# A list scheduler whose later work queues behind the last instruction of the first stage

## Chip, core and metric

One core of a Trainium2 chip runs the whole program. The metric is device time in microseconds of one execution, given as the median of the runs. Besides them one execution was profiled; its instruction records are the trace.

## What is computed

The reference is two layers of a diffusion backbone over 256 context and 256 latent tokens of width 1024 (512 rows of activations together). Each layer has a half-step feed-forward block, four token mixers side by side, and a second feed-forward block, each behind an RMS norm that is modulated by the conditioning vectors:

```python
def pre_norm(t, gain, m, i):
    return modulate(rms_norm(t, gain), m[..., 3 * i, :], m[..., 3 * i + 1, :])

def swiglu(h, w_up, w_down):
    a, g = jnp.split(h @ w_up, 2, axis=-1)
    return (jax.nn.silu(a) * g) @ w_down
...
# per layer: x + 0.5 * gate * swiglu(pre_norm(x)), then four mixers
# (gated DeltaNet, Hyena, Mamba-2 SSD, GLA), then the second feed-forward
```

The modulation `m` is the conditioning vector (one for context, one for latent) through a matrix `w_ada` of 1024 by 9 x 1024 per layer. The products run in float32 as three matmuls of split operands (high x high, high x low, low x high).

## The kernel before

The Python program does not emit instructions as it runs. A recording object (`Stand`) notes every operation with its engine, what it reads and writes, a modelled duration and a key, and `Plan.run` then lists them: on each of five queues (PE, DVE, ACT, POOL, SP) it takes at each modelled moment the operation with the smallest key among those whose inputs and buffers are ready. `build` emits the instructions in that order, and each engine runs its own queue strictly in order. All instructions are emitted by one statement, so the profile gives them line 585 (588 after the change), and tiles are told apart by name.

**The first stage** is `Kern.start` (line 792). It loads the tokens (`xin`, 8 transfers), transposes them, forms the RMS norm, and computes the modulation of the first norm in eight column blocks b0 to b7: four transfers `aw` of `w_ada` per block, 32 small matmuls (`px<-aw,cond`), an evacuation `adas`, two transposes, and three short DVE steps on the coefficients `c`. As block k is done, `norm_g` makes the normalised rows `hh` (ACT) and `hl` (POOL `v`, then DVE), and `up_mm(k)` issues the 12 matmuls of contraction block k of the first four column tiles of the feed-forward. Their weights come in four `raw` tiles of two transfers each (`load_w`); POOL makes the high part `wh`, DVE the low part `wl`. So the stage has 48 loads of 256 KB on SP and 96 matmuls of 512 columns. It ends with `up_evac`: `sil` (ACT), the product with the gate half (DVE), `ah` (ACT), `al` (DVE).

Within this stage the order on each queue is the order in which it is written: `manual_schedule` makes each operation depend on the one before it on its queue (`deps` of -1, which mean "not before it starts"; they order a queue and are no semaphore). When the block closes, `floor` is set to the recorder's clock, so everything stated later has a key that is no smaller. A key is only a priority, though: while the stage's next operation on a queue is not ready, a later one that is ready goes first.

**What is stated behind it** and is ready early: two small loads (`grp`, `cmats`); the generator `later()` in `body` (line 2477), with the Hyena filter inputs (`hy_load`, some thirty small transfers on the ACT queue together with `load_vA` and `load_layer`), the filter constants (`Fm`, `win`, `hywo`, `hyb` on SP) and the hidden layers of the filter network; the modulation of the other norms (`ada`, line 956), which streams `w_ada` in 256 KB tiles `aw` and accumulates them on DVE, eight steps `aa` per 512 KB; and the weights of the next feed-forward chunks (`wchunk`, line 686: one `raw` of 512 KB, `wh` on ACT, `wl` on DVE, three buffers of each), 24 matmuls of 512 columns a chunk.

The two lines that decide the order of all this are

```python
        if "SP" in self.strict:
            self.floor = self.t
...
        o.key = max(self.t - self.off[-1], self.floor)
```

Of the kernel before, what the change touches and what calls it, by code (L numbers as in the profile page):

```python
# [152 lines left out]
class Stand:  # L153
# [3 lines left out]
    def __init__(self, nc):  # L157
        self.real, self.shadow = nc, _bacc.Bacc("TRN2", target_bir_lowering=False, num_devices=1)
        self.ops, self.tiles, self.hist, self.dr = [], {}, {}, set()
        self.t, self.off, self.pe_last, self.maker = 0.0, [0.0], {}, {}  # L160
        self.strict, self.lead, self.floor = {}, 15.0, 0.0
        for a, e in self.ENG.items():
            setattr(self, a, self.Engine(self, e))

# [23 lines left out]
    @contextlib.contextmanager  # L188
    def manual_schedule(self, engines=None):

        self.strict = {NAMES[e]: None for e in engines}
        yield
        if "SP" in self.strict:
            self.floor = self.t
        self.strict = {}

    @contextlib.contextmanager
# [40 lines left out]
    def note(self, eng, name, args, kw):  # L238
        if name == "preload_act_table_set":
            return Note()  # L240
        o = Op()
        o.n, o.eng, o.name, o.args, o.kw = len(self.ops), eng, name, args, kw
        o.dma = name == "dma_start"
        o.deps, o.succ, o.new, o.tiles = {}, [], None, []
        aps = [x for x in list(args) + list(kw.values()) if isinstance(x, bass.AP)]
        o.func = None
        for x in list(args) + list(kw.values()):
            if isinstance(x, type(AF.Copy)):
                o.func = x
        for i, x in enumerate(aps):  # L250
            tn, w = x.tensor.name, i == 0
            if tn in self.tiles:
                b = self.box(x)
                if tn not in o.tiles:
                    o.tiles.append(tn)
                    if tn not in self.hist:
                        assert w, (tn, name)
                        o.new, self.maker[tn] = tn, o.n
                    else:

                        o.deps.setdefault(self.maker[tn], -1)
            elif tn in self.dr:
                b = self.dbox(x)
            else:
                continue
            self.access(o, tn, w, b, tn in self.dr)
            if w and eng == "PE":
                p = self.pe_last.get(tn)
                if p is not None:
                    o.deps[p] = max(o.deps.get(p, 0), 0)  # L270
                self.pe_last[tn] = o.n
        if eng in self.strict:
            if self.strict[eng] is not None:
                o.deps.setdefault(self.strict[eng], -1)
            self.strict[eng] = o.n
        for tn in o.tiles:
            self.tiles[tn][5] += 1
        self.cost(o, aps)
        o.key = max(self.t - self.off[-1], self.floor)
        if eng == "PE":  # L280
            self.t += o.occ / 1e3
        self.ops.append(o)
        return Note()
# [2247 lines left out]
```

## Time and profile before

| | |
|---|---|
| median of 3 runs | 2760.29 us (2759.2 to 2762.18) |
| profiled execution | 2761.68 us |
| its span, first to last instruction | 2759.9 us |
| PE busy, share of the span | 2661.1 us, 96% |
| DVE busy | 1910.1 us, 69% |
| ACT busy | 1043.5 us, 38% |
| POOL busy | 359.4 us, 13% |
| mean granted TensorE clock | 0.98 |

A busy PE here means that matmuls are in flight; the granted clock says at which of two speeds (1.0 is 2.4 GHz, 0.5 is 1.2 GHz). The 1.8 us between the profiled time and the span lie before the first and behind the last instruction. A wait is put down to the instruction or transfer that ended last before it.

### The profile page before, as it was taken

What the parts mean: (1) busy time and instruction counts of PE and PEld (TensorE: products, weight loads), DVE (VectorE), ACT (ScalarE), POOL (GpSimd) and SP (SyncE); (2) the same over time, 40 slices, a digit from 0 to 9 for tenths busy, and PEclk for the clock granted to TensorE, in tenths of its full rate; (3) what the DMA queues carried; (4) which work ended last, traced back from release to release, by engine and by line L of the source; (5) the groups of instructions that cost most, each with busy time, mean ns of one, the idle gap of its engine ahead of it and who ended that gap; (6) DMA issues with size and microseconds to landing.
All of it is one profiled execution on the core that took longest, in us unless ns stands there. A gap on an engine that the chain in (4) does not pass through costs nothing.

```text
span 2759.9 us, 40079 instructions
## 1 busy us (share of the span) xinstructions
PE 2661.1 (96%) x15131; PEld 2275.8 (82%) x15131; DVE 1910.1 (69%) x3783; ACT 1043.5 (38%) x1598; POOL 359.4 (13%) x439
## 2 busy tenths in 40 slices
PE   5999999999999999999999999999999899999998
PEld 3788877777989888887888878888878789999998
DVE  5968884778867565479737666556368987877555
ACT  2332222744433534233222233313246434644443
POOL 2200000201120242421000001000022112232000
PEclk6999999999999999999999999999999999999999
DMA  7745544232344233245534444444234435555454
GB/s 230 221 152 184 180 146 130 85 102 66 117 127 137 83 107 100 77 158 169 170 99 153 153 132 149 142 148 136 92 84 131 119 115 160 188 154 173 152 183 143
DMA packets 369697, 382.66 MB, mean 139 GB/s; under 512 B 43466, under 2 KB 317544, under 8 KB 369504
## 3 DMA queue, kind: packets, MB, share of 16 engines
q1 hardware_dynamic: 347568, 363.67, 43.3%
q10 hardware_dynamic: 21936, 16.44, 1.8%
q8 instruction: 119, 1.95, 0.3%
q14 instruction: 74, 0.61, 0.1%
HBM read 355.79 MB, written 24.25 MB: 138 GB/s over the span
## 4 chain that ended last, share of the span: by engine, by line
PE 83%; DVE 10%; DMA 3%; issue 1%; POOL 1%; ACT 1%; SPq 0%; ACTq 0%; DVEq 0%; POOLq 0%
PE pmm L585 72%; PE px L585 11%; DVE qkv L585 1%; DVE wl L585 1%; DVE X L585 1%; DVE P L585 1%; DVE xbc L585 1%; DVE aa L585 1%; DMA raw<-in_ffn_up 1%; DMA aw<-in_w_ada 0%; DVE u L585 0%; DMA gdr<-gA 0%; POOL bm L585 0%; POOL v L585 0%; DVE TC L585 0%
## 5 line engine op out<-in xcount | busy, mean ns | idle before, releaser
L585 DVE TENSOR_TENSOR wl<-raw,wh 128x1024 fp32r<-128x1024 f32 (+1 forms) x486 | 594.8, 1225 | 464.3 <-ACT wh L585 459.1
L585 ACT ACTIVATE wh<-raw 128x1024 fp32r<-128x1024 f32 (+1 forms) x480 | 502.0, 1046 | 1076.1 <-PE pmm L585 921.2
L585 PE MATMUL pmm<-hh,wh 128*128 128x512 f32 (+1 forms) x2464 | 896.2, 364 | 3.1 <-ACT hh L585 1.9
L585 PE MATMUL pmm<-hh,wl 128*128 128x512 f32 (+1 forms) x2464 | 886.7, 360 | 3.1 <-DVE wl L585 2.9
L585 PE MATMUL pmm<-hl,wh 128*128 128x512 f32 (+1 forms) x2464 | 885.2, 360 | 4.3 <-DVE hl L585 4.2
L585 PEld LDWEIGHTS pmm<-hh,wh 128*128 128x128 f32 x2464 | 469.4, 191 | 77.5 <-issue 8.6
L585 PEld LDWEIGHTS pmm<-hl,wh 128*128 128x128 f32 x2464 | 468.6, 190 | 74.8 <-DVE hl L585 7.1
L585 PEld LDWEIGHTS pmm<-hh,wl 128*128 128x128 f32 x2464 | 469.8, 191 | 70.5 <-DVE wl L585 4.4
L585 DVE SCALAR_TENSOR_TENSOR aa<-aw,cond,aa 128x256 f32<-128x256 f32 x896 | 369.8, 476 | 1.2 <-DMA aw<-in_w_ada 1.1
L585 PE MATMUL pmm<-ah,wh 128*128 128x512 f32 (+1 forms) x704 | 258.6, 367 | 0.0
L585 PE MATMUL pmm<-ah,wl 128*128 128x512 f32 (+1 forms) x704 | 256.4, 364 | 0.0
L585 PE MATMUL pmm<-al,wh 128*128 128x512 f32 (+1 forms) x704 | 256.2, 364 | 0.0
L585 PEld LDWEIGHTS pmm<-ah,wh 128*128 128x128 f32 x704 | 133.5, 190 | 23.0 <-issue 2.5
L585 PEld LDWEIGHTS pmm<-al,wh 128*128 128x128 f32 x704 | 133.3, 189 | 21.4 <-issue 0.4
L585 PEld LDWEIGHTS pmm<-ah,wl 128*128 128x128 f32 x704 | 133.5, 190 | 20.6
L585 PE MATMUL pmm<-wl,hh 128*128 128x256 f32 x416 | 119.7, 288 | 8.8 <-DVE wl L585 8.8
L585 PE MATMUL pmm<-wh,hh 128*128 128x256 f32 x416 | 120.3, 289 | 0.0
L585 PE MATMUL pmm<-wh,hl 128*128 128x256 f32 x416 | 119.6, 287 | 0.0
L585 POOL TENSOR_SCALAR v<-u,Am,mods 128x256 f32<-128x256 f32 x72 | 56.4, 804 | 466.9 <-DVE u L585 466.9
L585 PEld LDWEIGHTS pmm<-wl,hh 128*128 128x128 f32 x416 | 80.1, 193 | 9.4 <-DVE wl L585 9.0
L585 PE MATMUL pmm<-yh,wh 128*128 128x512 f32 (+1 forms) x256 | 87.8, 344 | 0.0
L585 PE MATMUL pmm<-yh,wl 128*128 128x512 f32 (+1 forms) x256 | 86.1, 338 | 0.0
(382 smaller groups left out, 3397.9 us busy)
## 6 DMA issues: line engine op xcount, KB each, us to landing
raw<-in_ffn_up SPq DMA_DIRECT2D x172, 512.0 KB
raw<-in_w_in SPq DMA_DIRECT2D x164, 512.0 KB
aw<-in_w_ada SPq DMA_DIRECT2D x288, 256.0 KB
raw<-in_ffn_down SPq DMA_DIRECT2D x80, 512.0 KB
raw<-in_w_branch SPq DMA_DIRECT2D x32, 512.0 KB
fe<-pk SPq DMA_DIRECT2D x42, 256.0 KB
raw<-in_w_out SPq DMA_DIRECT2D x16, 512.0 KB
pk<-pj ACTq DMA_DIRECT2D x26, 256.0 KB
```

The lines of the kernel that those rows point to most:

```text
L585: getattr(engines[o.eng], o.name)(*[sub(a) for a in o.args], **{k: sub(v) for k, v in o.kw.items()})
```

## The change

When the first stage closes, the recorder keeps the number of the last instruction that the stage put on each queue (`gates`). Every operation that is stated later gets a dependence of -1 on its own queue's one: the scheduler may not place it ahead of it. Nothing else is changed: keys, costs, buffers, the stage itself.

```diff
@@ -158,7 +158,7 @@
-        self.strict, self.lead, self.floor = {}, 15.0, 0.0
+        self.strict, self.lead, self.floor, self.gates = {}, 15.0, 0.0, {}
@@ -191,7 +191,8 @@
         self.strict = {NAMES[e]: None for e in engines}
         yield
         if "SP" in self.strict:
-            self.floor = self.t
+
+            self.floor, self.gates = self.t, dict(self.strict)
         self.strict = {}
@@ -269,6 +270,8 @@
                 self.pe_last[tn] = o.n
+        if self.gates.get(eng) is not None and eng not in self.strict:
+            o.deps.setdefault(self.gates[eng], -1)
         if eng in self.strict:
```

**SP, in the stage's loads.** Before, 18 transfers that belong to later work stand between the two halves of the stage's first weight tile (`raw_106`); these are the last ten of them, the second half, and the first load of block b1:

```order
L585 DMA cmats<-in_cmats 128x9x128
L585 DMA Fm_132<-in_dftF 128x512
L585 DMA win_134<-in_hywin 128x2x256
L585 DMA win_136<-in_hywin 128x2x256
L585 DMA hywo_138<-in_hy_wout 64x256
L585 DMA hywo_140<-in_hy_wout 64x256
L585 DMA hyb_144<-in_hy_bias 1x256
L585 DMA hyb_146<-in_hy_bias 1x256
L585 DMA hywo_138<-in_hy_wout 64x256
L585 DMA hywo_140<-in_hy_wout 64x256
L585 DMA raw_106<-in_ffn_up 128x2x256
L585 DMA aw_259<-in_w_ada 128x4x128
```

With the change the two halves (x2) stand together, behind the four loads of b0, and b1 and b2 follow at once:

```order
L588 DMA aw_99<-in_w_ada 128x4x128
L588 DMA raw_104<-in_ffn_up 128x2x256 x2
L588 DMA aw_225<-in_w_ada 128x4x128
L588 DMA aw_227<-in_w_ada 128x4x128
L588 DMA aw_229<-in_w_ada 128x4x128
L588 DMA aw_231<-in_w_ada 128x4x128
L588 DMA aw_233<-in_w_ada 128x4x128
```

Over the whole stage 32 transfers leave the places ahead of its last load: 17 `aw` tiles of 256 KB, 3 `raw` of 512 KB, `Fm` and `win` (4 of 256 KB), `cmats` (576 KB), `hywo` (4 of 64 KB) and three of a few KB.

**DVE, between two blocks of the stage.** Before, steps `aa` of the later modulation stand around the stage's `wl`, `c`, `u` and `hl` of one block:

```order
L585 SCALAR_TENSOR_TENSOR aa_352<-aw_391,cond_229,aa_352 128x256
L585 SCALAR_TENSOR_TENSOR aa_355<-aw_391,cond_229,aa_355 128x256
L585 TENSOR_TENSOR wl_578<-raw_277,wh_565 128x1024
L585 TENSOR_REDUCE c_588<-px_465 128x4
L585 TENSOR_TENSOR c_588<-c_588,vA_235 128x4
L585 TENSOR_SCALAR c_588<-c_588,vA_235 128x2
L585 TENSOR_TENSOR u_593<-x_239,px_449 128x512
L585 TENSOR_TENSOR hl_600<-v_574,hh_528 128x512
L585 SCALAR_TENSOR_TENSOR aa_358<-aw_391,cond_229,aa_358 128x256
```

With the change the same piece has none, and none stands anywhere in the stage:

```order
L588 TENSOR_TENSOR hl_366<-v_320,hh_317 128x512
L588 TENSOR_TENSOR wl_387<-raw_241,wh_375 128x1024
L588 TENSOR_REDUCE c_399<-px_299 128x4
L588 TENSOR_TENSOR c_399<-c_399,vA_170 128x4
L588 TENSOR_SCALAR c_399<-c_399,vA_170 128x2
L588 TENSOR_TENSOR u_406<-x_177,px_286 128x512
L588 TENSOR_TENSOR hl_411<-v_384,hh_361 128x512
```

88 steps `aa`, three `wl` of the next chunks, seven steps of the filter network and a copy of loaded rows move behind the stage's last DVE step.

**ACT, at the end of the stage.** Before, the first two splits of the next chunks (`wh_952`, `wh_1001`) stand among the stage's last evacuations, and all small transfers of `later()` far ahead of them:

```order
L585 ACTIVATE wh_952<-raw_671 128x1024
L583 ACT_TABLE_LOAD
L585 ACTIVATE sil_976<-pmm_505 128x512
L585 ACTIVATE sil_994<-pmm_540 128x512
L585 ACTIVATE wh_1001<-raw_737 128x1024
L585 ACTIVATE ah_1010<-sil_976 128x512
L585 ACTIVATE adas_1018<-px_870 128x256
L585 ACTIVATE ah_1038<-sil_994 128x512
```

With the change the splits stand behind the last evacuation, and the transfers between the splits that follow:

```order
L588 ACTIVATE ah_760<-sil_744 128x512
L588 ACTIVATE ah_765<-sil_751 128x512
L588 ACTIVATE wh_767<-raw_583 128x1024
L588 ACTIVATE wh_773<-raw_590 128x1024
L588 DMA hyz_783<-in_hyz 33x256
L588 DMA hyw_785<-in_hy_w 33x64
L588 DMA hyw_793<-in_hy_w 64x2x64
L588 DMA hyw_793<-in_hy_w 64x64
L588 ACTIVATE wh_809<-raw_665 128x1024
```

30 transfers now lie between `wh_773` and the split of the eighth chunk, `wh_1077`; 37 stood among the stage's instructions before. On PE two matmuls of the filter network, a transpose and seven picks (`px<-aa,pick`) move behind the stage, on POOL ten memsets. Behind the first feed-forward block the order on every queue is that of before, but for some dozens of neighbours that change places.

## Rows read from the trace of the kernel before

**Rows 1.** Busy time by stretch: PE, PEld, DVE, ACT, POOL (x), PEclk, DMA share, GB/s.

```profile
0.00:50.00 50.00, 20.29 (x136) 14.42 (x136) 21.38 (x56) 13.15 (x23) 10.20 (x25) 0.63 0.67 198
50.00:100.00 50.00, 42.47 (x307) 28.73 (x308) 43.11 (x102) 14.97 (x27) 23.03 (x18) 0.79 0.89 278
100.00:150.00 50.00, 50.00 (x221) 40.82 (x220) 48.50 (x101) 15.46 (x20) 0.00 (x0) 1.00 0.63 199
150.00:200.00 50.00, 50.00 (x223) 41.38 (x222) 28.60 (x51) 14.98 (x19) 0.00 (x0) 1.00 0.47 146
```

**Rows 2.** The chain that ended last, 0 to 110 us: start, us, what.

```profile
12.72 5.59 DMA raw<-in_ffn_up
18.33 8.29 DMA alog<-in_gdn_a_log
...
38.08 7.47 DMA aw<-in_w_ada
...
83.97 3.85 POOL wh L585
```

**Rows 3.** SP's queue: start, us, transfer.

```profile
35.73 0.59 SPq L585 DMA_DIRECT2D raw<-in_ffn_up  x1
```

**Rows 4.** Busy time by stretch, columns as in rows 1.

```profile
0.00:16.00 16.00, 7.35 (x31) 5.07 (x31) 3.97 (x8) 4.64 (x8) 6.00 (x20) 0.91 0.76 230
40.00:44.00 4.00, 0.66 (x8) 0.23 (x8) 0.00 (x0) 0.00 (x0) 1.04 (x1) 0.50 0.99 284
```

**Rows 5.** ACT's timeline: start, us, instruction, [idle before <- what ended it].

```profile
18.78 1.09 ACT L585 ACTIVATE sq<-px 128x512 f32<-128x512 f32 x2 [6.75 <-DMA rows<-in_gdn_conv]
```

**Rows 6.** PE's timeline through the stage to its last matmul.

```profile
23.64 3.54 PE L585 MATMUL px<-ones,acc 128*128 128x1 f32 x16 [2.23 <-DVE acc L585]
...
43.32 2.93 PE L585 MATMUL px<-aw,cond 128*32 128x128 f32 x32 [13.80 <-DMA aw<-in_w_ada]
...
52.26 0.80 PE L585 MATMUL pmm<-hh,wh 128*128 128x512 f32 x1
...
66.36 1.08 PE L585 MATMUL px<-aw,cond 128*32 128x128 f32 x32
...
70.59 0.43 PE L585 MATMUL px<-aw,cond 128*32 128x128 f32 x8
...
70.95 0.64 PE L585 MATMUL px<-hyh,hyw 64*64 64x256 f32 x2
...
75.89 0.80 PE L585 MATMUL pmm<-hl,wh 128*128 128x512 f32 x1 [2.19 <-DVE hl L585]
...
80.32 0.63 PE L585 MATMUL pmm<-hl,wh 128*128 128x512 f32 x1
...
100.22 0.39 PE L585 MATMUL pmm<-hl,wh 128*128 128x512 f32 x1
```

**Rows 7.** DVE's and ACT's steps of a gate product and of splits.

```profile
101.78 1.23 DVE L585 TENSOR_TENSOR wl<-raw,wh 128x1024 fp32r<-128x1024 f32 x1 [0.27 <-ACT wh L585]
...
103.53 0.68 DVE L585 TENSOR_TENSOR sil<-sil,pmm 128x512 f32<-128x512 f32 x1
...
104.24 0.63 ACT L585 ACTIVATE ah<-sil 128x512 fp32r<-128x512 f32 x1 [1.70 <-DVE sil L585]
...
228.34 1.06 ACT L585 ACTIVATE wh<-raw 128x1024 fp32r<-128x1024 f32 x1 [4.33 <-DVE aa L585]
233.78 1.06 ACT L585 ACTIVATE wh<-raw 128x1024 fp32r<-128x1024 f32 x1 [4.38 <-PE pmm L585]
```

**Rows 8.** PE's timeline in the feed-forward: a group of eight picks.

```profile
204.93 1.07 PE L585 MATMUL px<-aa,pick 128*32 128x256 f32 x16
```

**Rows 9.** ACT's queue: the first and the last of 37 small transfers of later work.

```profile
3.48 0.30 ACTq L585 DMA_DIRECT2D hyz<-in_hyz  x1
...
53.55 0.26 ACTq L585 DMA_DIRECT2D rows<-in_ssd_norm  x1
```

**Rows 10.** DVE's timeline: a run of modulation steps.

```profile
80.24 5.63 DVE L585 SCALAR_TENSOR_TENSOR aa<-aw,cond,aa 128x256 f32<-128x256 f32 x14
```

## The prediction

> **What bounds the kernel now.** The page's first line gives a span of 2759.9 us; the profiled execution took 2761.68, 1.4 above the median of 2760.29. I make the sum against the former and take the 1.4 off at the end. First read busy time by stretch [rows 1]: PE is busy for 20.3 of the first 50 us and 42.5 of the next 50, at a mean clock of 0.63 and 0.79; from 100 us on for 50.0 of 50 at full clock. The first stage is where PE waits, and the change acts there. The chain that ended last says why [rows 2]: from 12.72 us it runs through a `raw` of later work and through `alog`, a small transfer of later work on ACT's queue, 8.29 us, until SP could issue on; only at 38.08 does it reach a load of the stage. SP's queue has the second half of the first stage weight at 35.73 [rows 3], 23.0 us behind the start of that other `raw`, and PE stood 13.80 us for block b1 [rows 6]. Further on the chain passes POOL's `wh` with 3.85 us where it ran beside `aa` steps on DVE. So the moved work does not just fill gaps of the stage; it makes some of them.
>
> **The change, part by part.** First the stage's end without the moved work.
>
> *Loads.* The stage has 48 loads of 262 KB, 12.58 MB. In the first 16 us 230 GB/s moved [rows 4], 3.68 MB, just the 14 loads up to the first weight (3.67 MB). Block b1, four loads, now follows at once. A stretch with the stage's loads alone ran at 284 GB/s [rows 4], so b1 lands at 16 + 1.05 / 0.284 = 19.7 us and the last, b7, at 16 + 8.91 / 0.284 = 47.4, or at 54.7 with 230 GB/s.
>
> *The norm.* ACT stood 6.75 us before the row at 18.78, behind transfers of later work on its own queue [rows 5], in the middle of the sums of squares. That goes, and PE's norm matmuls, 23.64 to 27.2 [rows 6], end at 20.4. So b1's small matmuls, at 43.32 before, start at 20.4 rather than 19.7.
>
> *To the first weight matmul.* Before, from 43.32 to 52.26 [rows 6], 8.9 us; kept as it is: 29.3.
>
> *The eight blocks.* A chunk of 24 matmuls takes 233.78 - 228.34 = 5.44 us at full clock [rows 7], 0.227 each. Block 0 runs at half clock, 12 at 0.453 and two transposes, some 6.5 us, and I add 2.2 for a half-clock start of block 1. A block at full clock took 70.59 - 66.36 = 4.23 us [rows 6], its small matmuls included; five of them, 21.2. Blocks 6 and 7 have no small matmuls left: 12 matmuls and a little, 2.8 each, 5.6. Together 35.5, so the stage's last matmul is over at 64.8 instead of 100.4 (the row at 100.22 and one interval). b7 is needed at about 55, so loads and PE come out nearly even, and I take 66. **Gain 34.4 us.** Bounds: 60 with full clock from block 0 on; 77.5 if the stretch from 52.26 to 100.4 keeps its 48.2 us whole. I stay near the first, since the waits in that stretch are those named above.
>
> *The boundary.* The first `wh` of the next chunk now queues behind the last `ah`, and `wl` behind that. After the stage's last matmul come the gate product 0.68, `ah` 0.63, `wh` 1.06 and `wl` 1.23 [rows 7], 3.60 and with the handovers some 3.8 us, in which PE has two matmuls, 0.4: 3.4 lost. Before, nothing was lost there. After an idle 2.19 us PE ran at half clock from 75.89 to past 80.32, matmuls of 0.63 instead of 0.39 [rows 6]: 5 us for half as much work, 2.5 more. **5.9 us given back**; ends 3.4 and 8.
>
> *Work moved on PE.* Seven picks, two products of the filter network and a transpose stood in gaps and now stand in a full queue. Eight picks took 1.07 there [rows 8], one product 0.64 [rows 6], the transpose counts as a matmul of 0.4: **2.6 us**; the lower end is 0.
>
> *Work moved on DVE.* 88 steps `aa` of 0.40 in a run (5.63 for 14) [rows 10], 35 us, go into a stretch where DVE was busy for 48.5 of 50. Their cover is a lull: from 150 to 200 us it was busy for 28.6 of 50 [rows 1]. By the changed order DVE has, from the boundary up to the 23rd split, 199 `aa` (79.6), 23 `wl` (26) and some 11 us of gate products: 116 to 117. PE needs that split 22 chunks on, at 5.44: 119.7. So about 3 us to spare at the tightest place: **0**. By the 38th split as many `aa` are left as before. With the cover gone it would be up to 35 us.
>
> *Loads moved on SP.* 32 transfers, 7.9 MB, 27.9 us at 284 GB/s. The next two chunks' weights stand right behind the stage's last load; the third stands behind 2.6 MB more, 9.2 us, and is needed 10.9 us after the boundary. The loads are ahead of PE, so most of this lands while the stage still computes: **0**; ends 0 and 27.9. The Trainium skill speaks against this part: "DMA: Bandwidth & Descriptors", section "Rules for kernel authors", says to issue a DMA early and to wait for its semaphore late. By that rule the moved transfers are uncovered, and the whole gain would be spent on them; the trace shows the early issue as the cost [rows 2], as these transfers stood in line ahead of awaited ones.
>
> *Transfers moved on ACT.* 30 small ones now stand between the splits of chunks 2 and 8. Their issue takes 0.3 us and up [rows 9]. Seven chunks give ACT 38.1 us, less 2.1 for the first two splits, 6.4 for six more and 2.5 for four evacuations: 27.1, so 0.90 each are free. In the stage 37 of them went from 3.48 to 53.55 [rows 9], 1.36 each, with ACT's other work and full queues; at that, 30 x 0.46 = 14 us would be lost. The DMA share was 0.89 in the stage and is 0.63 behind it [rows 1], so I take **0**; ends 0 and 14.
>
> *POOL.* Ten memsets move behind its last stage step, where POOL has no work up to 200 us [rows 1]: 0.
>
> Sum: 34.4 - 5.9 - 2.6 = 25.9; 2761.7 - 25.9 = 2735.8, less 1.4 for the median: **2734.4 us**.
>
> **Rivals.** *ACT's queue starves PE a little.* A DMA issue can stand for earlier ones to land, as SP's did [rows 2]; at 1.2 to 1.36 us each 9 to 14 us go, and 2743 to 2748 is left. For it: the splits share that queue. Against: fuller queues then than now. *Slower*, at the same place, decided by the time per transfer: if each holds ACT for 1.95 us (30 x 1.05 = 31.5), the 25.9 are gone and 0.2% besides, 2766. One did stand for 8.29, but 1.36 on average with full queues speaks against. *Moved loads uncovered*: PE waits 27.9 us for `raw` in the first chunks, 2762. Against: PE's own work reaches to 66 us, the stage's loads to 55 at most. That is how it would go by the Trainium skill's rule named above. *Given back later*: `aa` steps run late and hold up DVE at the end of the feed-forward and at the next norm; 10 to 20 of their 35 us, 2745 to 2755. Against: the order behind that block is that of before. That the change does nothing is out: the order shows the moves.
>
> **How the numbers follow.** A measurement tells 0.2%, 5.5 us, from no change. The forecast with its bounds: 0.74. ACT a little late: 0.12. Given back later: 0.06, half of it within 5.5 us of before. Loads uncovered: 0.05, no change. Slower: 0.03. So faster 0.89, same 0.08, slower 0.03. Low end: a stage end of 60, 3.4 at the boundary, nothing on PE, 2723.3, taken as 2724. High end: ACT's 14 us with a stage end 4 us later, 2752.
>
> **What would show it.** SP: the stage weight's second half near 13 us, b7 issued by 50. PE: b1's small matmuls at 19 to 24, the first weight matmul near 30, the stage's last near 66, then a gap of 2.5 us and a short one, half clock for 5 us, and from there no wait to 400 us. POOL's `wh` near 1 us. All that follows is shifted as a whole. I am wrong if the stage ends behind 78 us, if PE waits for `wh` or `raw` between the boundary and 150 us, or if its waits behind 400 us grow by over 3 us.

## The result and the profile after

The changed kernel took 2733.07 us (median of 4 runs, 2732.03 to 2733.84) beside 2760.93 (4 runs) for the kernel before on the same chip: a ratio of 0.9899, 95% interval 0.9882 to 0.9916. That is 27.9 us less; 25.9 were forecast, and 2733.07 lies 1.3 us below the forecast of 2734.4. The profiled execution took 2733.53, with a span of 2731.4 us, 28.5 less than before. The steps were right in kind; two were off in size with opposite signs, and one came out partly by luck.

Busy time by stretch, after (columns: stretch, its length, busy us of PE, PE's weight load, DVE, ACT, POOL with the number of instructions, granted clock, DMA share, GB/s), beside [rows 1]:

```profile
0.00:50.00 50.00, 36.92 (x343) 28.67 (x344) 24.92 (x56) 15.45 (x32) 19.49 (x28) 0.86 0.99 302
50.00:100.00 50.00, 45.69 (x216) 36.44 (x215) 35.52 (x76) 18.20 (x28) 7.49 (x15) 0.93 0.58 174
100.00:150.00 50.00, 50.00 (x233) 40.21 (x232) 49.79 (x114) 16.73 (x22) 0.00 (x0) 1.00 0.67 212
150.00:200.00 50.00, 50.00 (x232) 40.10 (x231) 49.79 (x111) 12.78 (x17) 0.00 (x0) 1.00 0.68 210
```

In the first 50 us the loads run at 302 GB/s instead of 198, and PE works 36.9 us instead of 20.3. The lull of DVE from 150 to 200 us is filled (49.8 of 50), as the forecast had it for the 88 steps `aa`, and PE does not notice.

SP's queue, after (start, duration, what, how many):

```profile
9.09 1.63 SPq L588 DMA_DIRECT2D raw<-in_ffn_up  x2
10.76 7.65 SPq L588 DMA_DIRECT2D aw<-in_w_ada  x8
...
37.21 2.68 SPq L588 DMA_DIRECT2D aw<-in_w_ada  x4
```

Both halves of the first stage weight are issued by 10.7 us; the second stood at 35.73 before [rows 3]. The last block's loads are issued by 39.9. PE, after (an idle time before an instruction, and what ended it, in brackets):

```profile
20.59 1.93 PE L588 MATMUL px<-aw,cond 128*32 128x128 f32 x32
...
27.02 0.47 PE L588 MATMUL pmm<-hh,wh 128*128 128x512 f32 x1 [0.49 <-ACT hh L588]
...
30.80 0.80 PE L588 MATMUL pmm<-hl,wh 128*128 128x512 f32 x1 [2.77 <-DVE hl L588]
...
48.44 1.08 PE L588 MATMUL px<-aw,cond 128*32 128x128 f32 x32
52.65 1.08 PE L588 MATMUL px<-aw,cond 128*32 128x128 f32 x32
...
61.98 0.39 PE L588 MATMUL pmm<-hl,wh 128*128 128x512 f32 x1
66.11 0.88 PE L588 MATMUL pmm<-hh,wh 128*128 128x512 f32 x2 [3.75 <-ACT wh L588]
67.56 0.79 PE L588 MATMUL pmm<-hh,wl 128*128 128x512 f32 x1 [0.56 <-DVE wl L588]
68.15 0.63 PE L588 MATMUL pmm<-hl,wh 128*128 128x512 f32 x1
...
73.27 0.45 PE L588 MATMUL pmm<-hh,wh 128*128 128x512 f32 x1
```

Block b1's small matmuls start at 20.59, where they stood at 43.32 behind a wait of 13.80 us [rows 6]. Block 0 takes 8.8 us (27.02 to 35.80), blocks 1 to 5 take 4.21 each (52.65 - 48.44), and the stage is over at 62.2. Then comes the price: PE stands for `wh` and `wl`, 3.75 and 0.56 us, and up to 73.27 a matmul shows 0.63 us instead of 0.39, at a granted clock of 0.53 (columns as above):

```profile
66.11:73.27 7.16, 6.59 (x15) 4.76 (x16) 7.16 (x16) 1.96 (x2) 0.00 (x0) 0.53 0.61 179
```

All that lies further on is shifted as a whole. The kernel before, from 378 us to its end, and the one after, from 350:

```profile
378.00:2759.90 2381.90, 2320.29 (x13421) 2006.67 (x13419) 1620.15 (x3152) 938.23 (x1454) 325.61 (x396) 0.99 0.43 130
```

```profile
350.00:2731.40 2381.40, 2320.28 (x13420) 2007.11 (x13418) 1622.67 (x3152) 937.25 (x1454) 324.96 (x396) 0.99 0.43 130
```

The two rests are 2381.9 and 2381.4 us long, and PE is busy for 2320.3 in both. So nothing is given back later.

### The profile page after: what moved, and what is told of

Read it like the earlier page. It is cut to its first block, busy times and chain, and to the rows that moved or that the text cites. A ratio compares the mean times of both kernels' runs of the same rounds, so it can differ in the third digit from the quotient of the medians.

```text
span 2731.4 us, 40099 instructions
## 1 busy us (share of the span) xinstructions
PE 2652.9 (97%) x15131; PEld 2274.0 (83%) x15131; DVE 1910.5 (70%) x3783; ACT 1040.4 (38%) x1596; POOL 352.5 (13%) x439
## 4 chain that ended last, share of the span: by engine, by line
PE 69%; DVE 9%; POOL 1%; issue 1%; ACT 1%; DMA 0%; ACTq 0%; DVEq 0%; POOLq 0%; SPq 0%
PE pmm L588 60%; PE px L588 10%; DVE qkv L588 1%; DVE wl L588 1%; DVE X L588 1%; POOL v L588 1%; DVE P L588 1%; DVE xbc L588 1%; DVE aa L588 1%; POOL bm L588 0%; ACT wh L588 0%; DVE TC L588 0%; DVE u L588 0%; DVE Y L588 0%; ACT vn L588 0%
## 5 line engine op out<-in xcount | busy, mean ns | idle before, releaser
L588 ACT ACTIVATE ah<-sil 128x512 fp32r<-128x512 f32 (+1 forms) x88 | 49.3, 572 | 102.1 <-DVE sil L588 93.7
```

The source lines that it names most:

```text
L588: getattr(engines[o.eng], o.name)(*[sub(a) for a in o.args], **{k: sub(v) for k, v in o.kw.items()})
```

## The experiments

Six kernels are the changed one with one more condition on the gate; the line that this replaces is shown once. The last two have other edits. All were timed beside the kernel before on their chip: it took 2761.14 us on that of the runs with the gate on DVE, on ACT's transfers, on SP and on all transfers, and 2760.64 on that of the others. The last four columns are read from the one profiled execution of each kernel.

| gate | median us (range) | ratio, 95% interval | b1's small matmuls | first weight matmul | stage ends | GB/s, first 50 us |
|---|---|---|---|---|---|---|
| none (before) | 2760.93 | | 43.32 | 52.26 | 100.4 | 198 |
| DVE alone | 2755.69 (2752.28 to 2759.57) | 0.9983 (0.9973 to 0.9992) | 41.86 | 52.26 | 83.7 | 199 |
| ACT's transfers alone | 2743.43 (2741.14 to 2747.57) | 0.9942 (0.9927 to 0.9957) | 27.70 | 35.19 | 81.5 | 294 |
| SP alone | 2734.09 (2730.75 to 2735.15) | 0.9904 (0.9890 to 0.9919) | 25.45 | 36.40 | 69.0 | 224 |
| all (the change) | 2733.07 (2732.03 to 2733.84) | 0.9899 (0.9882 to 0.9916) | 20.59 | 27.02 | 62.2 | 302 |
| all but DVE | 2734.89 (2732.68 to 2736.41) | 0.9905 (0.9889 to 0.9922) | 21.39 | 27.21 | 61.7 | 316 |
| all transfers, nothing else | 2726.05 (2723.91 to 2727.02) | 0.9876 (0.9862 to 0.9891) | 20.57 | 27.01 | 61.4 | 312 |
| all but `wh` and `wl` | 2724.80 (2724.61 to 2727.33) | 0.9873 (0.9859 to 0.9888) | 20.12 | 26.56 | 62.2 | 323 |

Where the next matmuls follow without a gap, the stage's end is counted: from block 5 on as in the changed kernel, with the last 24 matmuls at 0.227 us.

### SP alone

```diff
-        if self.gates.get(eng) is not None and eng not in self.strict:
+        if eng == "SP" and self.gates.get(eng) is not None and eng not in self.strict:
```

> The gate holds for SP alone. Theory L (the gain of 28 us comes from transfers of later work that stood in line ahead of the stage's loads, most of it from SP's own 32): the stage weight's second half is issued by 14 us, but ACT's small transfers still stand among its squares, so b1's small matmuls start at 24 to 30 instead of 20.6 and the stage's last matmul ends at 67 to 75 instead of 62.2; the later splits may go ahead again, so the gap of 4.3 us at the boundary and the half clock behind it are gone (7.6 us back). Together 2730 to 2740. Rival A (ACT's small transfers are the main cause, through their wait on SP's queue of 8.29 us and the squares' 6.75): the stage ends behind 80, 2745 or more. Rival D (the 88 steps aa on DVE are the main cause): they can't run without their loads, so 2725 to 2735 too; this run does not tell D from L.

Measured: 2734.09 us. b1 at 25.45 and the stage's end at 69.0 lie in the ranges of theory L. The gap at the boundary is gone, since `wh` and `wl` go ahead again. So the 6.8 us that the stage is longer are about made up by the 7.5 that the boundary no longer takes, and the time equals that of the whole change. On ACT's queue the squares still stand behind a transfer, and PE's first weight matmul waits for the norm:

```profile
17.48 1.08 ACT L588 ACTIVATE sq<-px 128x512 f32<-128x512 f32 x2 [5.76 <-DMA hyv<-in_hy_freq]
```

```profile
36.40 0.76 PE L588 MATMUL pmm<-hh,wh 128*128 128x512 f32 x1 [4.25 <-ACT hh L588]
```

SP's queue holds nothing but the stage's loads in their right order, and still the loads come at 224 GB/s. Its waits in the first 65 us (sum, times, longest):

```profile
SPq L588 <- DMA aw<-in_w_ada: 14.9, 13, 3.7
SPq L588 <- DMA raw<-in_ffn_up: 4.6, 4, 2.7
```

With ACT's transfers held back too, in the whole change, the first of these is all but gone:

```profile
SPq L588 <- DMA aw<-in_w_ada: 0.4, 1, 0.4
```

### ACT's transfers alone

```diff
+        if eng == "ACT" and o.dma and self.gates.get(eng) is not None and eng not in self.strict:
```

> The gate holds for ACT's transfers alone. Theory L: the squares' wait of 6.75 us goes and so does SP's 8.29 us behind one of the small transfers, but 18 later transfers of SP still stand ahead of b1's loads and 14 more among the rest: b1's small matmuls at 31 to 38 instead of 43.3, the stage ends at 86 to 95 instead of 100.4, 2747 to 2756. Rival A: b1 near 24, stage end near 70, 2728 to 2738. Rival D: the aa steps are still in the stage, so the time of before less a few us, 2753 to 2760.

Measured: 2743.43 us, between the two theories; b1 and the stage's end come sooner than theory L had them. The 18 later transfers still stand ahead of b1 on SP, but they pass fast now:

```profile
14.08 0.33 SPq L588 DMA_DIRECT2D Fm<-in_dftF  x1
14.45 0.43 SPq L588 DMA_DIRECT2D cmats<-in_cmats  x1
15.79 0.80 SPq L588 DMA_DIRECT2D Fm<-in_dftF  x1
...
23.23 0.41 SPq L588 DMA_DIRECT2D raw<-in_ffn_up  x1
```

The weight's second half is issued at 23.23 instead of 35.73, and b1 starts 15.6 us sooner than before. I had expected 5 to 12. So ACT's small transfers cost SP's queue far more than their bytes. The two queues in the first 60 us of the kernel before, SP's and ACT's (packets, MB, share of the 16 engines' time):

```profile
q1 hardware_dynamic: 14986, 12.33, 66.7%
q10 hardware_dynamic: 4204, 0.46, 5.3%
```

From its first weight matmul on, though, this run's stage takes 46.3 us, nearly the 48.2 of before; the whole change takes 35.2. PE waits four times for `hl`, 1.98, 2.17, 1.46 and 1.74 us, where the whole change has one such wait. This is the part of rival D that holds. Runs of `aa` stand among DVE's work, POOL's `wh` takes 3.89 us beside one of them (1.04 to 1.05 in the whole change, which has none there), and `wl` and `hl` come late:

```profile
62.86 5.62 DVE L588 SCALAR_TENSOR_TENSOR aa<-aw,cond,aa 128x256 f32<-128x256 f32 x14
66.55 3.89 POOL L588 TENSOR_SCALAR wh<-raw 128x1024 fp32r<-128x1024 f32 x1 [7.42 <-DMA aw<-in_w_ada]
70.48 1.23 DVE L588 TENSOR_TENSOR wl<-raw,wh 128x1024 fp32r<-128x1024 f32 x1 [0.94 <-POOL wh L588]
73.36 0.50 PE L588 MATMUL pmm<-hl,wh 128*128 128x512 f32 x1 [1.74 <-DVE hl L588]
```

The two queues' parts do not add up. Against before, b1 comes 15.6 us sooner without ACT's transfers, 17.9 without SP's and 22.7 without both. The compiled program's listing says why. The transfers of both queues take eight semaphores in turn, and nearly every one in the stage waits until the transfer that had its semaphore last has landed. In the kernel before these three, on SP, ACT and SP, had the same one:

```
L585 DMA raw_110<-in_ffn_up 128x4x256 [waits DMAHW3_49]
L585 DMA alog_256<-in_gdn_a_log 128x2x4 [waits DMAHW3_49]
L585 DMA Fm_132<-in_dftF 128x512 [waits DMAHW3_49]
```

That is the chain of [rows 2] step by step: the `raw` from 12.72 us on, `alog` at 18.33 for 8.29 us, and SP's next issue at 26.63. A small transfer waits for a large one of the other queue, and the next large one for the small. Taking either party out ends most of it. How much of the stall is the turn-taking, and how much the slow landing of the small ones as such, was not separated.

### DVE alone

```diff
+        if eng == "DVE" and self.gates.get(eng) is not None and eng not in self.strict:
```

> The gate holds for DVE alone: no step aa is left in the stage. Because their tiles are then not freed, 12 of the 17 later loads aw are held back as well; the first 18 later transfers of SP and all of ACT's stay where they were. Theory L: b1's small matmuls start at 40 to 45 as before; from there on the stage runs with a few later loads in its way, some 4.3 to 5 us a block, and ends at 80 to 90; the later wl stand behind the stage's last DVE step, so half of the gap at the boundary stays. 2745 to 2758. Rival D: the aa steps were the cause, so most of the gain is here: 2728 to 2738.

Measured: 2755.69 us, in theory L's range. Rival D is out as the cause of most of the time: with no `aa` in the stage b1 is nearly as late as before, behind a transfer, and the first weight matmul as late to the hundredth:

```profile
41.86 0.65 PE L588 MATMUL px<-aw,cond 128*32 128x128 f32 x8 [11.13 <-DMA aw<-in_w_ada]
...
52.26 0.80 PE L588 MATMUL pmm<-hh,wh 128*128 128x512 f32 x1
...
89.40 0.80 PE L588 MATMUL pmm<-hh,wl 128*128 128x512 f32 x1 [2.02 <-DVE wl L588]
```

From there on the stage takes 31.4 us instead of 48.2, less than in any other run here, and PE waits for no `hl`. Two things are gone together: the `aa` steps, and 12 later loads whose tiles the held steps do not free. No run has one without the other, so what each is worth is not shown. Of the 16.7 us by which the stage is shorter, waits of 0.74, 1.34 and 2.02 us at the boundary, with half clock behind them, take some 7, and the work moved on PE some 2; the median is only 5.5 below that of before, so some 2 us stay open.

### All transfers, nothing else

```diff
+        if o.dma and self.gates.get(eng) is not None and eng not in self.strict:
```

> The gate holds for transfers alone, SP's and ACT's; nothing is held on DVE, PE, POOL or for ACT's arithmetic. Theory L: the stage as with the whole change (b1 at 20.6, last matmul at 62 to 64), and the splits wh and wl of the next chunks go ahead, so the gap of 4.3 us and 3.3 us of half clock are gone: 2724 to 2729. Rival D: aa steps may stand in the stage again and slow it: 2733 or more. Rival C (part of the gain comes from holding back the splits themselves, that is from ACT and DVE in the stage): 2731 to 2740, with b6 or b7 late by 1 to 3 us.

Measured: 2726.05 us, as theory L had it, 7.0 less than the whole change. The stage is that of the change to 0.8 us, the gap is gone, and PE is never idle from 50 to 100 us:

```profile
50.00:100.00 50.00, 50.00 (x251) 41.04 (x250) 42.28 (x89) 21.95 (x31) 3.92 (x4) 1.00 0.68 201
```

So holding back the two queues of transfers is enough for the whole gain. It keeps `aa` out of the stage as well, since their loads then come behind the stage's; this run does not tell the two apart.

### All but `wh` and `wl`

```diff
+        if aps[0].tensor.name.rstrip("0123456789") not in ("wh", "wl") and self.gates.get(eng) is not None and eng not in self.strict:
```

> The whole change, but the outputs wh and wl of later chunks are exempt from the gate; steps aa, transfers, picks and POOL's memsets stay held. Theory L (the boundary's gap comes from the splits alone): stage as with the change, last matmul at 62, no gap and no half clock behind it, 7.6 us less than the change's 2733.1: 2724 to 2728, the same as with the gate on transfers alone. Rival B (the gap is only shifted: the next chunks' raw or DVE's queue is late instead, and PE stops for it before 150 us): 2729 to 2733.

Measured: 2724.80 us, 8.3 less than the change, and the same as the last run within their ranges. On ACT two `wh` of the next chunks, at 55.11 and 57.29, stand ahead of the stage's last evacuations again:

```profile
57.29 1.05 ACT L588 ACTIVATE wh<-raw 128x1024 fp32r<-128x1024 f32 x1
60.34 1.28 ACT L588 ACTIVATE sil<-pmm 128x512 f32<-128x512 f32 x2 [2.01 <-PE pmm L588]
```

Rival B is out: its PE waits for nothing from 60 to 350 us. The boundary's price is that of the splits held back: 8.3 us by this run, and 7.0 by the one with the gate on all transfers, whose stage ends 0.8 sooner.

### All but DVE

```diff
+        if eng != "DVE" and self.gates.get(eng) is not None and eng not in self.strict:
```

> The whole change, but nothing is held on DVE; PE's order is that of the change to the last instruction. 8 steps aa stand ahead of the stage's first gate product and 9 more between the products and the first wl. Theory L (holding DVE earns nothing inside the stage, since the loads of aa come late anyway): the stage ends at 62 as with the change; at the boundary the products and so ah, wh and wl come up to 4 us later: 2733 to 2738. Rival D (holding aa back is what made the stage short): stage end behind 66, 2739 or more.

Measured: 2734.89 us, in theory L's range. The stage ends at 61.7 with DVE free to place `aa` in it, but none starts before 58.00, as their loads come behind the stage's; so this run says nothing of `aa` amid the stage. Eight steps stand ahead of the first gate product, and PE's gap grows from 3.75 to 5.70 us:

```profile
58.00 4.54 DVE L588 TENSOR_SCALAR aa<-aw,cond 128x256 f32<-128x256 f32 x8
62.47 0.67 DVE L588 TENSOR_TENSOR sil<-sil,pmm 128x512 f32<-128x512 f32 x1
63.07 1.66 DVE L588 SCALAR_TENSOR_TENSOR aa<-aw,cond,aa 128x256 f32<-128x256 f32 x4
```

```profile
67.59 1.22 PE L588 MATMUL pmm<-hh,wh 128*128 128x512 f32 x2 [5.70 <-ACT wh L588]
```

The 1.8 us between the medians is of that size, but the ranges overlap; it is the trace that shows the gap.

### Thirty more transfers on ACT behind the stage

```diff
-        self.strict, self.lead, self.floor, self.gates = {}, 15.0, 0.0, {}
+        self.strict, self.lead, self.floor, self.gates, self.twice = {}, 15.0, 0.0, {}, 0
...
         self.ops.append(o)
+        if self.gates and not self.strict and eng == "ACT" and o.dma and self.twice < 30 and aps[0].tensor.name in self.tiles and aps[0].ap[-1][1] > 2:
+            self.twice += 1
+            d = self.dram_tensor(f"tw{self.twice}", tuple(k for _, k in aps[0].ap), F32).ap()
+            self.note(eng, name, (d, aps[1]), {})
         return Note()
```

> The whole change, with 30 more small transfers on ACT's queue behind the gate: the first 30 of the later ones that move more than 2 elements a row are issued a second time, into scratch memory that nobody reads. This doses the term that I put at 0 with an upper end of 14 us. Theory L (a transfer behind the stage costs ACT 0.3 to 0.5 us, and 27 us are free in the next seven chunks, after which more chunks offer as much): PE waits nowhere for wh between the boundary and 200 us, 2732 to 2736. Rival A2 (ACT's queue was just short of its limit; each transfer stands 0.9 to 1.3 us for earlier ones): 2743 to 2765, with PE waiting for wh.

Measured: 2730.70 us (2729.57 to 2735.46), ratio 0.9896 (0.9881 to 0.9911): no cost. ACT does stand behind transfers, up to 6.91 us at once, and yet PE's waits from 60 to 350 us are those of the boundary alone:

```profile
74.53 1.06 ACT L592 ACTIVATE wh<-raw 128x1024 fp32r<-128x1024 f32 x1 [6.91 <-DMA hyw<-in_hy_w]
```

```profile
PE pmm L592 <- ACT wh L592: 3.8, 1, 3.8
PE pmm L592 <- DVE wl L592: 0.7, 1, 0.7
```

Three splits stand ahead of that wait, which gives PE some 16 us of work (3 x 5.44). The term I had put at 0 is 0 at twice the dose, but by this lead and not by short waits.

### The first `hl` sooner, with the gate on transfers

```diff
-        if self.gates.get(eng) is not None and eng not in self.strict:
+        if o.dma and self.gates.get(eng) is not None and eng not in self.strict:
...
-        ng = self.norm_g(lambda k: coef[k], 0, 512)
+        ng = self.norm_g(lambda k: coef[k], 0, 512, 2)
...
-        mod_t(1)
         load(3)
...
             next(ng)
+            if k == 0:
+                mod_t(1)
```

> The gate on transfers alone, and in the stage the first hl is stated ahead of two products u and of b1's coefficients, which stood before it on DVE; PE's order is unchanged. With the change, and with the gate on transfers, PE waits 2.8 us for this hl at 28 to 30.8 us and then runs at half clock to 35 us. Theory L: hl is there 1.5 to 2 us sooner, the wait is 1 us, b2 and all behind it are 2 to 3 us earlier: 2722.5 to 2725 against 2726.05 with the gate on transfers alone. Rival: block 1's hh or hl is late instead, by the coefficients that now come later: 2726 to 2728.

Measured: 2722.47 us (2720.93 to 2724.47), ratio 0.9863 (0.9849 to 0.9878), the fastest here: 10.6 less than the change, 38.2 less than before. PE's wait for this `hl` falls from 2.8 to 1.48 us:

```profile
29.55 0.56 PE L588 MATMUL pmm<-hl,wh 128*128 128x512 f32 x1 [1.48 <-DVE hl L588]
...
33.85 1.08 PE L588 MATMUL px<-aw,cond 128*32 128x128 f32 x32
```

The small matmuls of the block after start at 33.85, against 35.02 with the gate on transfers alone. The trace gives 1.2 us to this edit, less than the 2 to 3 expected; the medians differ by 3.6 with ranges that overlap, so more than the 1.2 is not shown.

## Why the prediction was right, point by point

**What bounds the stage.** It was read rightly from the chain of waits: transfers of later work in line ahead of awaited ones. Of the 38.2 us that the stage is shorter, 25.2 lie ahead of the first weight matmul (52.26 to 27.02), and those are shown to be SP's and ACT's transfers: with DVE alone held back that matmul stands where it stood. The other 13.0 lie behind it (48.2 to 35.2). There the forecast's last thread counts, POOL's `wh` beside `aa`: before, PE waited 2.19 us at 75.89 [rows 6] and 1.97 at 90.74 for `hl`, each behind a long `wh`, of 2.92 us in the row below and of 3.85 in [rows 2], and 2.9 for `aw` as well:

```profile
69.70 2.92 POOL L585 TENSOR_SCALAR wh<-raw 128x1024 fp32r<-128x1024 f32 x1 [6.55 <-DMA raw<-in_ffn_up]
```

```profile
90.74 0.50 PE L585 MATMUL pmm<-hl,wh 128*128 128x512 f32 x1 [1.97 <-DVE hl L585]
```

How these 13.0 divide between `aa` and the later loads is not shown. What the forecast did not see is that the two queues were one chain through their semaphores, and that 302 GB/s would run over 50 us; I had taken 284 and 230 [rows 4].

**The stage's end.** Said: 64.8, taken as 66. It is 62.2. b1's small matmuls start at 20.59 (20.4 said). The step that was off is "To the first weight matmul", kept at its 8.9 us of before: it takes 6.4 (27.02 - 20.59). The two groups of 32 small matmuls in it, spread over 2.86 and 3.33 us before by waits for single `aw` tiles, take 1.86 and 1.64, as b1 and b2 have landed; in the second the granted clock is 0.94 besides, where it was 0.50. That is 2.5, and the 1.2 for safety the rest. The eight blocks take 35.2 us (35.5 said), but their start came out by luck: 6.5 us of half clock for block 0 and 2.2 for a slow start of block 1 were said, 8.7 together. Block 0 did take 8.8, of which 2.77 are a wait for `hl` that was not foreseen, and block 1 began at full clock. Gain 38.2 instead of 34.4.

**The boundary.** Said: 3.4 idle and 2.5 of half clock, 5.9. Measured: 4.31 idle, and at half clock from 66.11 to 73.27 fifteen matmuls, which at 0.227 would take 3.4 of the 6.6 us that PE was busy: 3.2. Together 7.5; the two runs that let the splits go ahead take 7.0 and 8.3 less. The term was under-sized because it counted one gate product and one `ah`, where there are two in a row. DVE, after:

```profile
61.78 0.69 DVE L588 TENSOR_TENSOR sil<-sil,pmm 128x512 f32<-128x512 f32 x1 [3.22 <-PE pmm L588]
63.16 0.69 DVE L588 TENSOR_TENSOR al<-sil,ah 128x512 fp32r<-128x512 f32 x1 [0.69 <-ACT ah L588]
63.77 0.68 DVE L588 TENSOR_TENSOR sil<-sil,pmm 128x512 f32<-128x512 f32 x1
...
66.29 2.35 DVE L588 TENSOR_TENSOR wl<-raw,wh 128x1024 fp32r<-128x1024 f32 x2
```

The second product (`sil`, 63.77) stands behind the first `al`, which waits 0.69 us for ACT's `ah`. So the second `ah` and with it `wh` come late.

**Work moved on PE.** Said: 2.6. What is left over of the difference of the spans, 38.2 - 7.5 - 28.5, is 2.2. It lies ahead of 330 us: a group of picks stands at 328.82 where it stood at 357.30, 28.5 later. Up to there PE has seven picks and two products of the filter network more than before behind the stage, which by [rows 8] and [rows 6] take 0.94 and 1.28, together 2.2; the transpose comes later.

**The four terms put at 0.** DVE's 88 `aa` steps: PE is full from 74 to 350 us, so 0. The sum for it was tighter than it said: 23 `wl` at the 1.23 of [rows 7] are 28.3, not 26, which would leave 0.8 us to spare and not 3. (In a row they cost less; two take 2.35 in the last row above.) SP's moved loads: the same, no wait for `raw`. ACT's transfers: 0, and 0 at twice their number; ACT does stand 3.90 and 5.41 us for two of them in the changed kernel, at 86.45 and 92.92, and PE for none. POOL's moved memsets: 0, and its `wh` in the stage is short now:

```profile
45.30 1.05 POOL L588 TENSOR_SCALAR wh<-raw 128x1024 fp32r<-128x1024 f32 x1
```

The Trainium skill ("DMA: Bandwidth & Descriptors", section "Rules for kernel authors") would have a DMA issued early and its semaphore waited for late. The runs here speak against it for these transfers: the early issue is what cost, and held back (32 on SP, 30 of ACT's among the splits of the next chunks) they cost PE no wait.

**The rivals.** ACT's queue starving PE, the rival with most weight, fell with its own dose, and *slower* with it. Moved loads uncovered fell with PE's full stretch from 74 to 350 us, and given back later with the two equal rests above.

So 38.2 - 7.5 - 2.2 = 28.5 stands against 34.4 - 5.9 - 2.6 = 25.9. The forecast was close partly by luck: a gain 3.8 too small and a boundary 1.6 too cheap offset each other.

## What to carry to other kernels

In a scheduler that fills gaps, a transfer placed early is not free: it takes a place in a queue and a turn among the transfers in flight, and the next awaited one stands behind it. Hold transfers back by the stage, but let the few operations that the next stage needs first (here `wh` and `wl`) go ahead; the difference was 7 to 8 us of 35. Work that such a transfer feeds goes back with it: here that was `aa`, beside which POOL's `wh` was slow. When two causes sit in one chain, remove each by itself before giving either a share: here the single gains for b1, 15.6 and 17.9 us, came to 22.7 together.

## What was not expected of the hardware

ACT's queue, with 0.46 MB and 5.3% of the DMA engines' time in the first 60 us of the kernel before, held all transfers to 198 GB/s over 50 us, and to 224 with SP's order right; without its later transfers 294 were moved, and 302 to 329 with SP's order right too. And a PE stall of 4.3 us cost 7.5: behind it the matmuls came every 0.427 us instead of every 0.227, at a granted clock of 0.53 from 66.11 to 73.27. Last, POOL's `wh`, 1.04 us in most places, took 2.92 and 3.85 us before and up to 3.89 with the gate on ACT's transfers, each time beside a run of `aa` on DVE; one of 1.34 stood beside such a run too, so what decides it is not shown.
